# An encoder layer's merge: the sample's output product from the unsplit weight, row by row, and one turn of two tiles later

## The chip, the cores and the metric

The kernel runs on one core of a Trainium2 chip. The metric is the device time of one execution in microseconds (us), lower is better. Five engines work from queues of their own: TensorE (PE) multiplies into PSUM banks, VectorE (DVE), ScalarE (ACT) and GpSimd (POOL) do the elementwise work, and SyncE (SP) issues most of the transfers. Each engine takes its queue in order; semaphores hold an instruction back until its operands are there.

## The reference

One layer of an encoder for two groups: a prompt of 1024 tokens and a sample of 32 tokens with a cache of 512. What matters here is the end of the mixer and the beginning of the feed-forward part:

```python
merged = (g_a * (o_a.reshape(B, T, H_A * DV) @ w_proj_a)
          + g_b * (o_b.reshape(B, T, H_B * D_HB) @ w_proj_b))
x = x + gt1 * rms_norm(merged @ w_out, g_post_mix)
h2 = rms_norm(x, g_pre_ffn) * (1 + sc2) + sh2
f, new_conv = conv_ffn(h2, conv_state, w_up, conv_w, conv_b, w_down)
x = x + gt2 * rms_norm(f, g_post_ffn)
```

All data are float32 and the width is 1024. The change touches `merged @ w_out` for the 32 sample tokens, and the place of one transposition of normalised prompt rows for `h2 @ w_up`.

## The kernel before

The stages run in the order of `run` (L2188): `stage_merge` (L1509) follows the attention and precedes `stage_up` and `stage_down`.

**Precision.** A prompt product is made of three passes: each operand is split into a high and a low half (`hi` on ACT at L65, `lo` on DVE at L68), and `mm3` (L70) adds high x high, high x low and low x high. A sample product instead takes the operands as plain float32.

**The merge, row by row.** The merged activations are kept transposed, as eight rows `m` of 128 channels by 1056 tokens (1024 of the prompt, 32 of the sample at the end). The loop at L1532 makes for each `m`:

- the gates, loaded into tiles `t` and passed through a sigmoid (L1538, L1539), the branch B product loaded and multiplied in (L1544, L1545);
- the branch A product on PE, three blocks of 352 columns with twelve products each (`mtile`, L1550), multiplied by its gate and added (L1552, L1553);
- the split of the row into `mh` and `ml` (L1554, L1555), and a copy of its 32 sample columns into a tile `gs` (L1556, L1557), of which there are two buffers;
- the load of 128 rows of `w_out` into a tile `wr` (L1561) and its split into `dh`/`dl` (or `dr`) by `dsplit` (L1562). `wr` has two buffers for all weights of this stage: the branch A projections (L1367), `w_out` and the first up-projection weights (L1690).

**The output product of the prompt.** `natural` (L1434) makes, for token tile `t` and column half `h`, one bank `s` (three buffers) over a group of rows. Rows 0 and 1 come behind m=2 (their results are copied into the accumulators `facc`), rows 2 and 3 half behind m=4 and half behind m=6 (added to `facc` by DVE at L1460), rows 4 to 7 at the end (L1642). The last call begins the first three (t, h) with rows 4, 5 and 6, and adds row 7 to each of them afterwards.

**The output product of the sample.** `natural_s` (L1466) takes the copies `gs` as the small operand (128x32) and both halves of the split weight, read as float32, as the wide one. Its 1024 result columns are laid out as four blocks of 256 on partitions 0, 32, 64 and 96 of one bank, `pv` (one buffer). It is called three times: rows 0 and 1 (copied to `facc[8]`), rows 2 and 3 (added), rows 4 to 7 (added; called from `natural` after (t, h) = (1, 0)). Then `done(8)` (L1604) normalises the sample: ACT squares, PE sums over partitions (L321), POOL takes the root, DVE scales and adds the residual, and the same again for the next norm, up to the transposition at L1674.

**The turns.** `done(t)` (L1597) sums the squares of a finished prompt tile on ACT, `resid` (L1629) scales it and adds the residual, and leaves the normalised tile in `xn`. `turned(t0)` (L1586) is a generator: each of its two steps transposes half of the channels of two tiles on PE (`norm_2`, L1660) into two banks `tr` (two buffers), which ACT empties (L1666). A step is taken where `next` is called. After the last tile, `up_half` (L1711) begins the up-projection: four groups `(b, i)` of twelve products, in the order (0,0), (0,1), (1,0), (1,1), and after each it calls its function `then` (L1718). The step's PE instructions are bound to stand behind the product that was issued last (L1593).

**The order of the queues.** The kernel is written in a framework that traces the operations and then orders each engine's queue at compile time, by the order of the program and by estimates of when operands are ready; a later operation that is ready may be put ahead of an earlier one that isn't. `issue_after` binds an order by hand. So the position of an instruction in its queue follows from the program, buffers and estimates, and is fixed when the kernel runs.

Of the kernel before, what the change touches and what calls it, by code (L numbers as in the profile page):

```python
# [8 lines left out]
F32 = mybir.dt.float32  # L9
# [3 lines left out]
ALU = mybir.AluOpType  # L13
# [6 lines left out]
KT = 8  # L20
# [24 lines left out]
class K:  # L45
# [1417 lines left out]
                if (t, h) == (1, 0) and done:  # L1463
                    sample()

    def natural_s(self, facc, lhs, ws, first, done=None):  # L1466

        nc = self.nc
        ps = self.bank("pv")
        mm = [(x, w) for x, wl in zip(lhs, ws) for w in wl]  # L1470
        for i, (x, w) in enumerate(mm):
            for j in range(4):
                nc.tensor.matmul(ps[32 * j : 32 * j + 32, :256], x, w[:, j * 256 : j * 256 + 256],
                                 start=i == 0, stop=i == len(mm) - 1)
        if first:
            nc.scalar.copy(facc[8], ps[:, :256])
        else:
            nc.vector.tensor_tensor(facc[8], facc[8], ps[:, :256], ALU.add)
        if done:
            done(8)  # L1480

    def new_facc(self, pool):
        return [pool.tile([P, D] if t < 8 else [P, 256], F32, name=self.nm("facc")) for t in range(9)]
# [25 lines left out]
    def stage_merge(self):  # L1509
        nc, a = self.nc, self.a  # L1510
        E = self.E = self.tc.alloc_tile_pool(name="acc", bufs=1, reuse_waits="tile")
        facc = self.facc = self.new_facc(E)
        E3 = self.E3 = self.tc.alloc_tile_pool(name="work", bufs=2, reuse_waits="tile")
        m0 = [self.tl(E3, [P, T], F32R, g) for g in ("mh", "ml")]
        X = self.tc.alloc_tile_pool(name="m3", bufs=1, side="right", reuse_waits="tile")
        xh, xl = self.xh, self.xl
        lhs, lhs_s, ws = [], [], []

        def drop(n):
            del lhs[:n], lhs_s[:n], ws[:n]  # L1520

        def nat_s(n, first=False, done=None):
            b = lambda x: x.bitcast(F32)
            self.natural_s(facc, lhs_s[:n], [(b(h), b(l)) for h, l in ws[:n]], first, done)

        def nat(n, first=False, done=None):
            if not done:
                nat_s(n, first)
            self.natural(facc, lhs[:n], ws[:n], first, done, lambda: nat_s(n, first, done))
            drop(n)  # L1530

        for m in range(KT):  # L1532
            mc = slice(m * P, (m + 1) * P)
            h, l, banks = self.pa.pop(0) if self.pa else (*self.split_proj(self.w_proj_a(m) if m > 2 else self.w2), [])
            gs = []
            for s in (0, 1):
# [12 lines left out]
            banks = [(*b, ps) for b, ps in zip(blks, banks)]  # L1549
            for c0, n, ps in chain(banks, self.mtile(h, l, xh, xl, blks[len(banks) :], 4, {1: "tr", 2: "tr mm mm"}.get(m, "mm tr"))):  # L1550
                c = slice(c0, c0 + n)
                nc.vector.tensor_tensor(ga[:, c], ps[:, :n], ga[:, c], ALU.mult)  # L1552
            nc.vector.tensor_tensor(ga, ga, gb, ALU.add)  # L1553
            self.hi(mh, ga)  # L1554
            self.ml = self.lo(ml, ga, mh).ins  # L1555
            ms = self.tl(E3, [P, TS], F32, "gs")  # L1556
            nc.vector.tensor_copy(ms, ga[:, TP:T])  # L1557
            lhs.append((mh, ml))
            lhs_s.append(ms)
            raw = self.tl(self.W, [P, D], F32, "wr")  # L1560
            nc.sync.dma_start(raw, a["w_out"][0, mc])  # L1561
            ws.append(self.dsplit(E3, raw, "dh dl" if m % 4 < 3 else "dr dr"))  # L1562
            if m == 2:
                with self.tc.issue_after(self.pe):
                    nat(2, True)
            elif m in (4, 6):
                self.natural(facc, lhs[:2], ws[:2], False, tiles=range(2 * m - 8, 2 * m - 4))
                if m == 6:
                    nat_s(2, False)
                    drop(2)  # L1570
        X.release()
        self.Op.release()

        H = self.Hp = self.tc.alloc_tile_pool(name="h2", bufs=1, side="right", reuse_waits="tile")
        self.B1h, self.B1l, self.B2h, self.B2l = (H.tile([P, 4, HC], F32R, name=self.nm("B")) for _ in range(4))
        Fp = self.Fp = self.tc.alloc_tile_pool(name="h2f", bufs=1, side="right", reuse_waits="tile")
        self.f2 = Fp.tile([P, KT, HC], F32, name="f2")
        G = self.tl(E3, [P, UW], F32, "t")[:, :D]
        tmp = self.tl(E3, [P, UW], F32, "t")[:, :D]
        Gs = self.tl(E3, [P, 256], F32, "Gs")  # L1580
        xs, tmps = self.tl(E3, [P, 256], F32, "Gx", 1), self.tl(E3, [P, 512], F32, "hf")[:, :256]
        self.quarters(xs, a["x_sample"][0])
        self.gate_rows(0, "g_post_mix", G, Gs, tmp, tmps)
# [12 lines left out]

        def done(t, h=1):  # L1597
            f = facc[t]
            if self.turn2:
                if next(self.turn2, self) is self:  # L1600
                    self.turn2 = None
            if h == 0:
                return
            if t == 8:  # L1604
                self.post(f, self.rstd_s(f, E3), Gs, xs)
                nc.gpsimd.dma_start(self.x1s, f)
                nc.vector.tensor_scalar(xs, f, self.rstd_s(f, E3), None, ALU.mult)
                self.norm_2(8, [xs], E3)
                return
            rs.append(self.rstd(self.sumsq(f, P, E3, "jk", 512), D, P))  # L1610
            if t == 1:
                raw = [self.w_up(0), self.w_up(NCH)]
                with self.tc.issue_after(self.ml):
                    self.up_set = [self.wsplit(x) for x in raw]
            if t:
                with self.tc.issue_after(self.added[1]):
                    resid(t - 1)
                if t > 2 and t % 2:
                    self.turn2 = turned(t - 3)
            if t == 7:  # L1620

                first = ((self.B1h, self.B1l), (self.B2h, self.B2l))
                turn = self.turn2
                self.first = [self.up_half(self.up_set[0], first, ("mm", "mm"), lambda b, i: i and next(turn, None))]
                resid(7)
                turn = turned(6)
                self.first.append(self.up_half(self.up_set[1], first, ("s", "s"), lambda b, i: b + i == 1 and next(turn)))

        def resid(t):  # L1629
            f = facc[t]  # L1630
            x = self.tl(E3, [P, UW], F32, "t")[:, :D]
            nc.sync.dma_start(x, a["x_prompt"][0, t * P : (t + 1) * P])
            self.post(f, rs[t], G, x, None)
            nc.sync.dma_start(self.x1d[t], f)
            r = self.rstd(self.sumsq(f, P, E3, "jk", 512), D, P)
            if t < 6:
                self.hi(x, f, r)
            else:
                nc.vector.tensor_scalar(x, f, r, None, ALU.mult)
            xn.append(x)  # L1640

        nat(4, False, done)  # L1642
        E3.release()
        E.release()
# [608 lines left out]
```

## Time and profile before

| | |
|---|---|
| time, median of 3 runs (lowest to highest) | 1718.38 us (1718.2 to 1720.1) |
| the profiled execution's own time | 1721.95 us |
| its span | 1720.2 us |
| mean granted TensorE clock | 0.996 |

The span is the time from the first to the last instruction of the profiled execution; a chain or a timeline is read in times from its start. How busy PE, its weight loads (PEld), DVE, ACT and POOL are in three stretches of the stage, by the view of windows (us of busy time):

| stretch | length | PE | PEld | DVE | ACT | POOL | granted clock |
|---|---|---|---|---|---|---|---|
| 881 to 977: rows 1 to 7 and the output product's early parts | 96.0 | 94.92 | 79.30 | 65.99 | 43.83 | 0.75 | 1.00 |
| 977 to 1018.5: the last output products and the turns | 41.5 | 40.67 | 32.96 | 30.25 | 28.10 | 13.70 | 1.00 |
| 1018.5 to 1036: the first up products and the last turns | 17.5 | 16.21 | 15.62 | 12.60 | 13.51 | 6.52 | 1.00 |

In the rows of a timeline the columns are start, duration, engine, line, operation, result and operands, shape and count; a bracket gives the idle time of the engine before the instruction and what ended it. A matmul's duration there is its whole passage through the array; the next one may start before it has ended, so the distance from start to start is what a stream of them costs.

### The profile page before, as it was taken

What the parts mean: (1) busy time and instruction counts of PE and PEld (TensorE: products, weight loads), DVE (VectorE), ACT (ScalarE), POOL (GpSimd) and SP (SyncE); (2) the same over time, 40 slices, a digit from 0 to 9 for tenths busy, and PEclk for the clock granted to TensorE, in tenths of its full rate; (3) what the DMA queues carried; (4) which work ended last, traced back from release to release, by engine and by line L of the source; (5) the groups of instructions that cost most, each with busy time, mean ns of one, the idle gap of its engine ahead of it and who ended that gap; (6) DMA issues with size and microseconds to landing.
All of it is one profiled execution on the core that took longest, in us unless ns stands there. A gap on an engine that the chain in (4) does not pass through costs nothing. (4 is left out here: it accounts for less than half of the span.)

```text
span 1720.2 us, 29533 instructions
## 1 busy us (share of the span) xinstructions
PE 1681.7 (98%) x11444; PEld 1535.0 (89%) x11444; DVE 1201.8 (70%) x1960; ACT 904.3 (53%) x1730; POOL 276.0 (16%) x586
## 2 busy tenths in 40 slices
PE   6999999999999999999999999999999999999998
PEld 3899999999999989989789789999999999977886
DVE  4576475574663587878586679887787787788456
ACT  5455454454544677776683376444444444544442
POOL 2211111211110011111100131211121111110013
PEclk8999999999999999999999999999999999999999
DMA  8243333342431222222165530524323323697753
GB/s 324 81 132 108 106 110 87 97 127 74 135 117 56 80 80 74 65 61 73 63 255 157 176 135 26 178 93 129 129 93 130 129 93 129 228 338 243 233 150 120
DMA packets 169309, 224.15 MB, mean 130 GB/s; under 512 B 12901, under 2 KB 115504, under 8 KB 169168
## 3 DMA queue, kind: packets, MB, share of 16 engines
q1 hardware_dynamic: 153552, 178.43, 32.8%
q0 software_dynamic: 15392, 43.74, 7.2%
q8 instruction: 90, 1.47, 0.4%
q14 instruction: 51, 0.42, 0.1%
q10 hardware_dynamic: 224, 0.09, 0.0%
HBM read 169.92 MB, written 51.77 MB: 129 GB/s over the span
## 5 line engine op out<-in xcount | busy, mean ns | idle before, releaser
L65 ACT ACTIVATE wh<-wr 128x1024 fp32r<-128x1024 f32 (+6 forms) x156 | 131.6, 854 | 250.8 <-PE s L1707 78.0
L68 DVE TENSOR_TENSOR wl<-wr,wh 128x1024 fp32r<-128x1024 f32 (+5 forms) x153 | 149.1, 981 | 129.1 <-ACT wh L65 129.0
L72 PE MATMUL mm<-hh,wh 128*128 128x352 f32 x688 | 232.0, 337 | 0.0
L73 PE MATMUL mm<-hl,wh 128*128 128x352 f32 x688 | 224.4, 326 | 0.4 <-DVE hl L291 0.4
L74 PE MATMUL mm<-hh,wl 128*128 128x352 f32 x688 | 224.4, 326 | 0.0
L72 PEld LDWEIGHTS mm<-hh,wh 128*128 128x128 f32 x688 | 130.3, 189 | 8.9 <-issue 4.9
L73 PEld LDWEIGHTS mm<-hl,wh 128*128 128x128 f32 x688 | 130.2, 189 | 3.8 <-DVE hl L291 1.7
L74 PEld LDWEIGHTS mm<-hh,wl 128*128 128x128 f32 x688 | 129.9, 189 | 0.8 <-issue 0.8
L68 DVE TENSOR_TENSOR PTl<-tr,PTh 128x512 fp32r<-128x512 f32 x96 | 65.6, 687 | 46.4 <-ACT PTh L65 45.7
L1706 PE MATMUL s<-T,wh 128*128 128x256 f32 (+1 forms) x328 | 93.5, 285 | 0.4 <-DVE u L1783 0.3
L1708 PE MATMUL s<-T,wl 128*128 128x256 f32 (+1 forms) x328 | 93.6, 285 | 0.0
L1707 PE MATMUL s<-T,wh 128*128 128x256 f32 (+1 forms) x328 | 93.2, 284 | 0.0
L1847 DVE SCALAR_TENSOR_TENSOR u<-u,c,u 128x1058 f32<-128x1058 f32 x68 | 87.1, 1318 | 2.0 <-ACT u L1844 0.7
L591 PE MATMUL tr<-c,A 128*128 128x128 f32 x576 | 83.8, 273 | 1.0 <-DVE os L1357 0.3
L65 ACT ACTIVATE PTh<-tr 128x512 fp32r<-128x512 f32 x96 | 57.0, 598 | 49.0 <-PE tr L591 48.9
L1708 PE MATMUL tr<-T,wl 128*128 128x272 f32 (+1 forms) x272 | 77.7, 285 | 0.4 <-DVE wl L68 0.4
L1706 PE MATMUL tr<-T,wh 128*128 128x272 f32 (+1 forms) x272 | 77.8, 286 | 0.0
L1707 PE MATMUL tr<-T,wh 128*128 128x272 f32 (+1 forms) x272 | 77.4, 285 | 0.0
L591 PEld LDWEIGHTS tr<-c,A 128*128 128x128 f32 x576 | 68.1, 140 | 6.4 <-issue 1.8
L68 DVE TENSOR_TENSOR wl<-S,wh 128x1024 fp32r<-128x1024 f32 x40 | 49.0, 1224 | 35.1 <-ACT wh L65 35.1
L1708 PE MATMUL mm<-T,wl 128*128 128x256 f32 (+1 forms) x256 | 73.0, 286 | 0.3 <-DVE wl L68 0.2
L1706 PE MATMUL mm<-T,wh 128*128 128x256 f32 (+1 forms) x256 | 73.1, 286 | 0.0
(688 smaller groups left out, 5341.7 us busy)
## 6 DMA issues: line engine op xcount, KB each, us to landing
wr<-in_w_ada_dram SPq DMA_DIRECT2D x48, 512.0 KB, 4.7
wr<-in_w_up_dram SPq DMA_DIRECT2D x44, 512.0 KB, 4.2
dr<-in_w_down_dram SPq DMA_DIRECT2D x43, 512.0 KB, 5.7
wr<-in_w_in_dram SPq DMA_DIRECT2D x33, 512.0 KB, 4.5
wr<-gdn SPq DMA_DIRECT2D x30, 512.0 KB, 4.2
gdn<-u POOLq DMA_DIRECT2D x23, 512.0 KB, 5.4
gd<-nat POOLq DMA_DIRECT2D x48, 176.0 KB, 2.3
t<-gd SPq DMA_DIRECT2D x16, 528.0 KB, 5.2
```

The costliest lines, as they stand in the source:

```text
L65: self.nc.scalar.activation(out, in_, AF.Identity, scale=scale)
L68: return self.nc.vector.tensor_tensor(out, full, hi.bitcast(F32), ALU.subtract)
L72: m(ps, lh, rh, start=start, stop=False)
L73: m(ps, lh, rl, start=False, stop=False)
L74: self.pe = m(ps, ll, rh, start=False, stop=stop).ins
L591: self.nc.tensor.transpose(tr[:, (2 * s + q) * P : (2 * s + q + 1) * P], at[q][:, b * P : b * P + P], self.idt)
L1706: m(ps[:, :n], w[0][:, k], x[0][:, k, c], start=first and k == 0, stop=False, skip_group_check=True)
L1707: m(ps[:, :n], w[0][:, k], x[1][:, k, c], start=False, stop=False, skip_group_check=True)
L1708: i = m(ps[:, :n], w[1][:, k], x[0][:, k, c], start=False, stop=k == 3, skip_group_check=True)
L1847: nc.vector.scalar_tensor_tensor(y, u[:, w : w + YW], self.cvT[:, w, cc : cc + 1], y, ALU.mult, ALU.add)
```

## The change

1. The sample's output product uses the loaded float32 tile `wr` itself instead of its two halves. It is made in eight parts, one for each row `m` directly behind the load of its weight, all into one bank `pv` that stays open from m=0 to m=7. The calls for groups of rows, the two additions to `facc[8]` and the early copy go; one copy of the finished bank to `facc[8]` on ACT comes, at the place where the last group was called.
2. In the first `up_half`, the two steps of the turn of tiles 4 and 5 are taken after groups (1,0) and (1,1) instead of (0,1) and (1,1): the first of them twelve products later.

```diff
-    def natural_s(self, facc, lhs, ws, first, done=None):
-
-        nc = self.nc
-        ps = self.bank("pv")
-        mm = [(x, w) for x, wl in zip(lhs, ws) for w in wl]
-        for i, (x, w) in enumerate(mm):
-            for j in range(4):
-                nc.tensor.matmul(ps[32 * j : 32 * j + 32, :256], x, w[:, j * 256 : j * 256 + 256],
-                                 start=i == 0, stop=i == len(mm) - 1)
-        if first:
-            nc.scalar.copy(facc[8], ps[:, :256])
-        else:
-            nc.vector.tensor_tensor(facc[8], facc[8], ps[:, :256], ALU.add)
-        if done:
-            done(8)
+    def natural_s(self, m, x, w):
+
+        if m == 0:
+            self.ns = self.bank("pv")
+        for j in range(4):
+            self.nc.tensor.matmul(self.ns[32 * j : 32 * j + 32, :256], x, w[:, j * 256 : j * 256 + 256],
+                                  start=m == 0, stop=m == KT - 1)
...
+        def sample():
+            nc.scalar.copy(facc[8], self.ns[:, :256])
+            done(8)
 
         def nat(n, first=False, done=None):
-            if not done:
-                nat_s(n, first)
-            self.natural(facc, lhs[:n], ws[:n], first, done, lambda: nat_s(n, first, done))
-            drop(n)
+            self.natural(facc, lhs[:n], ws[:n], first, done, sample)
+            del lhs[:n], ws[:n]
...
             raw = self.tl(self.W, [P, D], F32, "wr")
             nc.sync.dma_start(raw, a["w_out"][0, mc])
+            self.natural_s(m, ms, raw)
             ws.append(self.dsplit(E3, raw, "dh dl" if m % 4 < 3 else "dr dr"))
...
                 if m == 6:
-                    nat_s(2, False)
-                    drop(2)
+                    del lhs[:2], ws[:2]
...
-                self.first = [self.up_half(self.up_set[0], first, ("mm", "mm"), lambda b, i: i and next(turn, None))]
+                self.first = [self.up_half(self.up_set[0], first, ("mm", "mm"), lambda b, i: b and next(turn, None))]
```

More of the change, by code (lines that the diff above doesn't have):

```diff
@@ L1516, in stage_merge @@
         xh, xl = self.xh, self.xl
[L1517 to L1524, printed above, removed]
+        lhs, ws = [], []
+        def sample():
+            nc.scalar.copy(facc[8], self.ns[:, :256])
+            done(8)
         def nat(n, first=False, done=None):
-            if not done:
-                nat_s(n, first)
-            self.natural(facc, lhs[:n], ws[:n], first, done, lambda: nat_s(n, first, done))
-            drop(n)
+            self.natural(facc, lhs[:n], ws[:n], first, done, sample)
+            del lhs[:n], ws[:n]
         for m in range(KT):
@@ L1558, in stage_merge @@
             lhs.append((mh, ml))
-            lhs_s.append(ms)
             raw = self.tl(self.W, [P, D], F32, "wr")
             nc.sync.dma_start(raw, a["w_out"][0, mc])
+            self.natural_s(m, ms, raw)
             ws.append(self.dsplit(E3, raw, "dh dl" if m % 4 < 3 else "dr dr"))
```

## The prediction

> **What bounds the kernel now.** I read the page's busy shares first, then the time order of TensorE (PE) through the merge stage, 881 to 1036 us, then its waits in that stretch.
>
> ```profile
> span 1720.2 us, 29533 instructions
> ```
>
> ```profile
> PE 1681.7 (98%) x11444; PEld 1535.0 (89%) x11444; DVE 1201.8 (70%) x1960; ACT 904.3 (53%) x1730; POOL 276.0 (16%) x586
> ```
>
> PE is busy for 98% of the span, so what counts is how long PE's queue is and where PE stands in it. Work taken off the vector engine (DVE) or ScalarE (ACT) is worth something only where PE waits for it.
>
> ```profile
> PE tr L1660 <- ACT t L65: 0.9, 1, 0.9
> PE s L74 <- DVE ml L68: 0.7, 1, 0.7
> PE tr L321 <- ACT hf L319: 0.5, 1, 0.5
> ```
>
> These are the three longest entries of PE's waits between 866 and 1045 us. The first is the transposition that the last hunk of the change moves. The second is the first product of row m=7, waiting for its low half. The third belongs to the sample's normalisation. Three small waits in 180 us: the stage is a nearly unbroken stream of products, and the sum has to come from the stream.
>
> **The change part by part.**
>
> *The sample's product.* Its instructions now, grouped by operand:
>
> ```profile
> L1473 PE MATMUL pv<-dh,gs x48: 379/379/404, 885.3 to 975.3; 128*32 128x256 f32 x48
> L1473 PE MATMUL pv<-dl,gs x48: 379/379/379, 885.7 to 975.7; 128*32 128x256 f32 x48
> L1473 PE MATMUL pv<-dr,gs x32: 379/379/379, 956.4 to 976.6; 128*32 128x256 f32 x32
> ```
>
> 48 + 48 + 32 = 128 instructions. The code has 8 rows m, two weight halves (high and low) and four column blocks, 64 calls, so each float32 call is two instructions. After the change each row multiplies the loaded weight once: 32 calls, 64 instructions. The 379 ns are not the price, since four blocks run in the array side by side; the price is the distance from one eight to the next:
>
> ```profile
> 973.13 0.61 PE L1473 MATMUL pv<-dl,gs 128*32 128x256 f32 x8
> 973.56 0.61 PE L1473 MATMUL pv<-dh,gs 128*32 128x256 f32 x8
> 974.00 0.61 PE L1473 MATMUL pv<-dl,gs 128*32 128x256 f32 x8
> 975.01 0.42 PE L1473 MATMUL pv<-dh,gs 128*32 128x256 f32 x4 [0.40 <-DVE gs L1557]
> ```
>
> Two eights lie between 973.13 and 974.00, so 0.87 / 16 = 0.054 us for one instruction. The 64 that go are worth 64 x 0.054 = 3.5 us.
>
> But entering and leaving the 32-column form costs something each time. A block of sixteen:
>
> ```profile
> 884.84 0.32 PE L73 MATMUL mm<-V,wh 128*128 128x352 f32 x1
> 885.00 0.32 PE L74 MATMUL mm<-V,wl 128*128 128x352 f32 x1
> 885.25 0.64 PE L1473 MATMUL pv<-dh,gs 128*32 128x256 f32 x8
> 885.71 0.61 PE L1473 MATMUL pv<-dl,gs 128*32 128x256 f32 x8
> 886.25 0.50 PE L72 MATMUL s<-dh,mh 128*128 128x512 f32 x1
> 886.59 0.39 PE L73 MATMUL s<-dl,mh 128*128 128x512 f32 x1
> 886.82 0.39 PE L74 MATMUL s<-dh,ml 128*128 128x512 f32 x1
> ```
>
> A product of 352 columns takes 0.16 us to the next start (884.84 to 885.00), one of 512 columns 0.23 (886.59 to 886.82). Without the block, the second product after it would have started at 885.00 + 0.16 + 0.23 = 885.39; it started at 886.59. The block cost 1.20 us, of which 16 x 0.054 = 0.86 is work and 0.34 is the two changes. The new blocks have eight instructions of the very form that the conditioning product already runs alone:
>
> ```profile
> 343.42 0.64 PE L203 MATMUL mm<-wr,cT 128*32 128x256 f32 x8
> 343.99 0.43 PE L72 MATMUL mm<-hh,wh 128*128 128x352 f32 x1
> 344.26 0.32 PE L73 MATMUL mm<-hl,wh 128*128 128x352 f32 x1
> ```
>
> 0.57 to the next start, 0.27 - 0.16 = 0.11 more to the one behind, and the 0.09 of entering seen above (885.25 against 885.16): 0.77 us, that is 0.43 of work and again 0.34. Now the stage has four blocks: two of sixteen (m = 0 and 1), one of 32 (m = 2, 3) and one of 64 (m = 4 to 7) with a wait in its middle. Afterwards each row is ready at another time, so I count eight. Four more blocks cost 4 x 0.34 = 1.4 us. Net: -3.5 + 1.4 = **-2.1**.
>
> That each change of form costs 0.34 us is measured above. The Trainium skill has a rule that speaks against this change here: changing the tiling mode, and not just the tile, drains TensorE (TensorEngine Tiling (Array Packing), Key Properties). It gives no price; by it every one of the eight blocks pays on both sides, however short, as the rows show for eight and for sixteen. Had the finer cut cost nothing, the net of this part would be -3.5.
>
> *The wait in the middle.* In the rows above, the eight at 975.01 should have started at 974.43: 0.58 us late, waiting for the copy of a sample row (gs). That tile has two buffers, both held by rows 4 and 5 until the products at 972 to 974. In the new form a row's product runs right behind its copy and the buffers come free early. **-0.6.**
>
> *The wait for m=7.* PE stood 0.7 us before that row's third product. Up to there it had done three sample blocks, 64 x 0.054 + 3 x 0.34 = 4.5 us; afterwards it will have done seven or eight, 5.4 or 6.2 us. PE comes 0.9 to 1.7 us later to a wait of 0.7. The low half itself gets no later:
>
> ```profile
> 967.18 1.06 ACT L65 ACTIVATE wh<-wr 128x1024 fp32r<-128x1024 f32 x1 [2.19 <-DMA wr<-in_w_up_dram]
> 968.15 1.07 ACT L65 ACTIVATE mh<-t 128x1056 fp32r<-128x1056 f32 x1
> ```
>
> The high half of row 7 (mh) stands in ACT's queue behind the split of the second up-projection weight, which waits 2.19 us for its load. That load will come later (below) and its split falls behind mh. **-0.7.**
>
> *New waits.* Each of the eight blocks now follows directly on a copy of DVE's, and PE is in order: where DVE is late, the projection and output products behind wait too. Below lies 0. Above, the largest wait of the stage, 0.9, eight times: 7.2. The nearest row is L1473 itself: five starts now, one of them 0.58 late. 8 / 5 x 0.58 = **+0.9** is the value I take.
>
> *The held weight buffer.* The loaded float32 tile (wr, two buffers, shared with the projection and up weights) is now read by PE, so it stays until the row's sample copy exists; so far it went free after the split.
>
> ```profile
> 903.81 0.38 SPq L1367 DMA_DIRECT2D wr<-in_w_proj_a_dram  x1
> ...
> 960.12 0.38 SPq L1690 DMA_DIRECT2D wr<-in_w_up_dram  x1
> ```
>
> ```profile
> 918.23 0.17 DVE L1557 COPY gs<-t 128x32 f32<-128x32 f32 x1
> ```
>
> ```profile
> DMA to landing us min/median/max: 3.4/3.9/6.0
> ```
>
> The projection weight of m=5 went out at 903.81. With both buffers held by w_out of rows 3 and 4 it goes out when row 3's sample copy (918.23) has been used, near 919; with at most 6.0 to land and some 1.4 to split it is there by 926.5, and PE's products of m=5 begin here:
>
> ```profile
> 932.65 0.32 PE L72 MATMUL mm<-QH,wh 128*128 128x352 f32 x1
> ```
>
> Rows 6 and 7 have room of the same kind. What is late is the second up weight: it needs the buffer of w_out 7, so it goes out near 969 in place of 960.12. Its products come in the second up half, just ahead of the turn at 1030.12 shown further below. I cost the hold at nothing, covered by these margins; the case without cover is a rival below. The loads queued behind it on SyncE (gain rows, residual rows) keep their own order of readiness and are no earlier than now.
>
> *The open bank.* The sum stays in bank pv from row 0 to the copy:
>
> ```profile
> L605 PE MATMUL pv<-ptd,V x256: 277/281/481, 96.2 to 872.9; 128*128 128x256 f32 x128
> ```
>
> The attention's last use of it starts at 872.9, before row 0's block, and the stage asks for it nowhere else: nothing. Two DVE adds and one early ACT copy go, one late ACT copy comes; neither engine bounds PE there.
>
> *The transposition twelve products later.*
>
> ```profile
> 1021.38 0.27 PE L1660 MATMUL tr<-c,t 128*128 128x128 f32 x1
> 1022.52 0.33 PE L1660 MATMUL tr<-c,t 128*128 128x128 f32 x1 [0.87 <-ACT t L65]
> ...
> 1024.81 1.91 ACT L1666 ACTIVATE f<-tr,c,c 128x256 f32<-128x256 f32 x4
> ...
> 1029.19 0.75 DVE L1639 TENSOR_SCALAR t<-facc,rs 128x1024 f32<-128x1024 f32 x1 [1.00 <-POOL rs L98]
> ...
> 1030.12 0.27 PE L1660 MATMUL tr<-c,t 128*128 128x128 f32 x1
> ```
>
> Twelve products of 0.12 us put these transpositions near 1022.9, and tile 5, ready at 1022.5, is no longer waited for. But PE then has only twelve products, not twenty-four, before the second half of the same turn, which needs the two tr banks that ACT empties from 1024.81 to 1026.7; and behind that, tile 7 is ready at 1029.94 for transpositions that now start at 1030.12. Both lie on ACT, DVE and GpSimd and don't move. The 0.9 becomes two smaller waits: I take **0**, with -0.9 and +0.5 as ends (another half microsecond if the banks are freed in a worse order).
>
> **The sum.** -2.1 - 0.6 - 0.7 + 0.9 + 0 = -2.5 us. The profiled execution took 1721.95 us, its span is 1720.2; it would become 1719.5. The median shown is 1718.38, 3.6 below the profiled one; the same 2.5 off gives **1715.9**. That is 0.15%; about 0.2%, or 3.4 us, is what a measurement of this kernel can tell from no change.
>
> **The rivals.**
>
> *All of it pays.* No block waits, and PE's earlier arrival at the turn is used. For it: few waits in this stage, seven of eight turns without one now. Against it: tile 7's chain. -2.1 - 0.6 - 0.7 - 0.9 = -4.3: 1714.1.
>
> *The wait takes the place of the work.* Every block finds its copy 0.58 late, as the one at 975.01: 8 x 0.58 = 4.6 in place of 0.9: +1.2, 1719.6. For it: the copies stand in DVE's queue among whole-row operations. Against it: four of five starts have no such wait.
>
> *The held buffer stops the tail: slower.* The second up weight goes out near 969. The load of 960.12 was used at 967.18, 7.0 us later; so ACT splits it from 976 and DVE ends the low half near 978.2. If that split keeps its place in DVE's queue, ahead of the output product's additions, the first of three s banks comes free at 978.9, while PE, past (0,0), (0,1) and (1,0), wants a fourth bank. Now it takes it here:
>
> ```profile
> 976.87 0.50 PE L72 MATMUL s<-dh,mh 128*128 128x512 f32 x1
> ```
>
> Without the block of 64 and its wait (64 x 0.054 + 0.34 + 0.58 = 4.4) that is 972.5, with up to 1.7 for the earlier blocks and without the 0.7 it is 973.5: 5.4 us of standing, and with ACT's squares behind the same load about a microsecond more. -2.5 + 6.5 = +4.0: 1722.4. It decides from about 6 us of standing. Against it: the order of a queue is set by estimated readiness, so the split should move behind the additions; only an estimate several microseconds short would leave it there.
>
> *It doesn't do what it says*: blocks could fall together again. Each pair saves 0.34, so even four pairs give -3.9, 1714.5, and this counts with the first rival.
>
> **How the numbers follow.** Forecast 0.47, all pays 0.25, wait in place of work 0.16, held buffer 0.12. Around the forecast the spread of the waits (0 to 2) goes from -3.4 to -1.4, and a sixth of it may pass -3.4: 0.08 goes to faster. Faster by over 0.2%: 0.25 + 0.08 = 0.33. Slower: 0.12. Within: 0.55. The range takes in the first rival with a little room (1713.3) and the second (1719.6), and leaves out the held buffer and the far edge of the first, together under 2 in 10.
>
> **What would show it.** Right: 64 instructions on the sample product in eight blocks near 0.77 us; no wait of PE for gs longer than 0.6; none for ml; the transposition near 24 + 12 products without its 0.87, and a new wait at the next turn or at tile 7. Wrong: blocks with waits of half a microsecond each; ACT or DVE standing for the up weight while PE waits for s banks; or later stages in another order than now, which this sum leaves out.

## The result, and the profile after

The changed kernel takes 1722.44 us (median of 22 executions), the kernel before 1719.88 us (median of 22, measured beside it). The ratio is 1.0016, with a 95% interval of 1.0009 to 1.0023. Three later measurements gave 1.0004 (0.9995 to 1.0013), 1.0010 (1.0001 to 1.0019) and 1.0013 (1.0004 to 1.0022); the mean of the four is 1.0011, or 1.9 us. So the change makes the kernel slower by about a tenth of a per cent. The forecast was 1715.9 us, faster by 2.5. Of the 6.5 us between forecast and result, 1.5 are the base (the three times shown gave 1718.38 for before, 22 give 1719.88), 2.5 are the gain that did not come, and the rest is a loss that was not foreseen.

The page of the profile after. Its execution took 1721.36 us, 1.1 below the median of its kernel; that of the profile before took 1721.95, 2.1 above. So these two traces alone do not show the loss:

```profile
span 1719.6 us, 29413 instructions
...
PE 1679.8 (98%) x11380; PEld 1532.2 (89%) x11380; DVE 1201.8 (70%) x1958; ACT 903.9 (53%) x1730; POOL 280.0 (16%) x586
```

11444 instructions of PE have become 11380: the 64 are gone. PE is busy 1.9 us less, and the span is 0.6 us shorter. GpSimd (POOL) does the same 586 instructions in 4.0 us more. That small number is where the trail below leads.

The four longest of PE's waits from 866 to 1045 us in the trace after (total, times, longest):

```profile
PE tr L1646 <- ACT f L1652: 1.1, 2, 0.8
PE tr L1646 <- ACT hf L1652: 1.1, 2, 0.8
PE tr L321 <- ACT hf L319: 0.6, 2, 0.4
PE tr L1660 <- DVE Gx L1593: 0.5, 1, 0.5
```

Lines behind the changed code stand 14 lower than before (L1646 is the transposition that was L1660). The waits for ml, for gs and for tile 5 are gone. In their place stand two waits of a new kind: PE has the tile, but the bank that the transposition needs has not been emptied by ACT. One of them is at the second step of the turn of tiles 4 and 5, at 1025 us, as the prediction had it; the other is in the first turn, at 1000 us, where before had none. A wait of 0.3 us for the high half of row 1 is new as well.

### The profile page after: what moved, and what is told of

Read it like the earlier page. It is cut to its first block, busy times and chain, and to the rows that moved or that the text cites. A ratio compares the mean times of both kernels' runs of the same rounds, so it can differ in the third digit from the quotient of the medians.

```text
span 1719.6 us, 29413 instructions
## 1 busy us (share of the span) xinstructions
PE 1679.8 (98%) x11380; PEld 1532.2 (89%) x11380; DVE 1201.8 (70%) x1958; ACT 903.9 (53%) x1730; POOL 280.0 (16%) x586
```

## Where the time went

*The blocks came out as forecast.* Row 0's block in PE's timeline after, and the group of all eight:

```profile
883.88 0.32 PE L72 MATMUL mm<-KH,wh 128*128 128x352 f32 x1
884.13 0.64 PE L1471 MATMUL pv<-wr,gs 128*32 128x256 f32 x8
884.70 0.43 PE L73 MATMUL mm<-KL,wh 128*128 128x352 f32 x1
884.97 0.32 PE L74 MATMUL mm<-KH,wl 128*128 128x352 f32 x1
```

```profile
L1471 PE MATMUL pv<-wr,gs x64: 379/391/403, 884.1 to 967.0; 128*32 128x256 f32 x64
```

From 883.88 to 884.97 are 1.09 us, where two plain products take 2 x 0.16: the block cost 0.77, the forecast figure, 0.43 of them work. 64 instructions in eight blocks, none waiting in this trace.

*PE did reach the turns 2.5 us earlier.* All traces start differently (the first 45 us, which wait for loads, differ by up to 3.6 us between executions of the kernels here), so I compare stretches, called the stage from here on: from the start of one of PE's last products of the attention, near 870 us, to the start of the sixteenth product behind the turn of tiles 4 and 5, near 1029 us. In a second trace of before these start at 869.98 and 1028.96: the stage is 158.98 us long. In its first trace it is 159.17. In three of four traces of the changed kernel it is 158.91, 158.89 and 158.86: no shorter. But up to the last product ahead of 1000 us the same three traces are ahead of that second trace of before by 2.5 to 2.6 us, as the sum said. The gain was there, and was lost between 1000 and 1029 us. The first place, in PE's timeline after and before:

```profile
998.80 0.40 PE L74 MATMUL s<-dr,ml 128*128 128x512 f32 x1
1000.01 0.66 PE L1646 MATMUL tr<-c,t 128*128 128x128 f32 x4 [0.82 <-ACT hf L1652]
1000.92 0.66 PE L1646 MATMUL tr<-c,t 128*128 128x128 f32 x4 [0.26 <-ACT hf L1652]
```

```profile
1002.05 1.04 PE L1660 MATMUL tr<-c,t 128*128 128x128 f32 x8
```

Before, the second step of this turn took its eight transpositions in one piece; now it stands twice. PE is 2.5 us ahead in front of this step and 1.0 behind it, and 0.8 behind the second turn. The second place is the turn of tiles 4 and 5: the wait for tile 5 is gone, which gives 0.8, but the turn's second step takes 1.5 more than before, and 0.1 is left:

```profile
1025.29 0.66 PE L1646 MATMUL tr<-c,t 128*128 128x128 f32 x4 [0.84 <-ACT f L1652]
1026.20 0.66 PE L1646 MATMUL tr<-c,t 128*128 128x128 f32 x4 [0.25 <-ACT f L1652]
```

*Why ACT was not earlier at the first turn.* ACT empties the banks (hf) in its own order, behind the scaling of tile 2 (t), which needs that tile's rs from GpSimd. ACT's timeline after:

```profile
990.84 0.19 ACT L105 ACTIVATION_READ_ACCUMULATOR jk<-facc 128x1 f32 x1
...
993.77 1.15 ACT L65 ACTIVATE t<-facc,rs 128x1024 f32<-128x1024 f32 x1 [1.56 <-POOL rs L98]
...
995.77 0.19 ACT L105 ACTIVATION_READ_ACCUMULATOR jk<-facc 128x1 f32 x1
...
997.90 1.15 ACT L65 ACTIVATE t<-facc,rs 128x1024 f32<-128x1024 f32 x1 [1.94 <-POOL rs L98]
998.96 1.91 ACT L1652 ACTIVATE hf<-tr,c,c 128x256 f32<-128x256 f32 x4
```

and before:

```profile
993.01 0.19 ACT L105 ACTIVATION_READ_ACCUMULATOR jk<-facc 128x1 f32 x1
994.14 1.15 ACT L65 ACTIVATE t<-facc,rs 128x1024 f32<-128x1024 f32 x1 [0.94 <-POOL rs L98]
...
997.33 0.19 ACT L105 ACTIVATION_READ_ACCUMULATOR jk<-facc 128x1 f32 x1
998.46 1.15 ACT L65 ACTIVATE t<-facc,rs 128x1024 f32<-128x1024 f32 x1 [0.94 <-POOL rs L98]
999.52 1.92 ACT L1666 ACTIVATE hf<-tr,c,c 128x256 f32<-128x256 f32 x4
```

From the end of a row's sum of squares to its scaling: before 994.14 - 993.20 = 0.94 and 998.46 - 997.52 = 0.94; after 993.77 - 991.03 = 2.74 and 997.90 - 995.96 = 1.94. The two gaps are 1.8 and 1.0 us longer. So the chain was 2.2 us ahead of before at the first sum (990.84 against 993.01) and only 0.6 at hf; 0.3 of either is this stage's earlier start, and ACT has one sum less to do between the two steps, or nothing would be left. GpSimd's two small operations lie in those gaps. GpSimd's timeline after, and DVE's beside it:

```profile
984.09 0.55 POOL L98 TENSOR_TENSOR rs<-rv,c 128x1 f32<-128x1 f32 x1
...
991.11 1.01 POOL L97 TENSOR_SCALAR rv<-ss 128x1 f32<-128x1 f32 x1 [0.36 <-ACT jk L105]
992.20 1.53 POOL L98 TENSOR_TENSOR rs<-rv,c 128x1 f32<-128x1 f32 x1
...
996.32 1.55 POOL L98 TENSOR_TENSOR rs<-rv,c 128x1 f32<-128x1 f32 x1
```

```profile
983.87 0.68 DVE L1460 TENSOR_TENSOR facc<-facc,s 128x512 f32<-128x512 f32 x1
...
990.79 1.28 DVE L1498 SCALAR_TENSOR_TENSOR facc<-facc,rs,t 128x1024 f32<-128x1024 f32 x1
992.11 1.23 DVE L1499 TENSOR_TENSOR facc<-facc,t 128x1024 f32<-128x1024 f32 x1
...
996.18 1.28 DVE L1498 SCALAR_TENSOR_TENSOR facc<-facc,rs,t 128x1024 f32<-128x1024 f32 x1
```

Both operations work on one column. The second (L98) takes 0.55 us when it runs alone and 1.53 when DVE has just begun one of its residual operations, which read two tiles of SBUF: it ends 0.4 us after DVE's (993.73 against 993.34, 997.87 against 997.46). The first (L97) takes 0.19 alone, and here 1.01: it ends 0.05 us after DVE's (992.12 against 992.07). Beside DVE's addition from a bank (983.87) the second takes 0.55. Before, the same two steps begin ahead of DVE's operation and take 0.19 and 0.55:

```profile
993.28 0.19 POOL L97 TENSOR_SCALAR rv<-ss 128x1 f32<-128x1 f32 x1 [0.36 <-ACT jk L105]
993.56 0.55 POOL L98 TENSOR_TENSOR rs<-rv,c 128x1 f32<-128x1 f32 x1
```

```profile
993.65 1.28 DVE L1506 SCALAR_TENSOR_TENSOR facc<-facc,rs,t 128x1024 f32<-128x1024 f32 x1
```

The Trainium skill names the rule (SBUF — State Buffer, SBUF: two separate sides): DVE's second pair of ports is shared with GpSimd, as an exclusive lock for a whole instruction, and an operation of DVE with two SBUF inputs takes it. The trace agrees as to GpSimd's waiting, the case with a bank among the inputs too. That DVE would in its turn wait for GpSimd these rows do not show: DVE's operation at 993.65 begins while GpSimd's of 993.56 runs, and takes the 1.28 us of the others. Between 974 and 1031 us, 4 of GpSimd's small operations take over 1.0 us in both traces of before, 7 in all four of the changed kernel. Three of the seven are those above, and they cost 0.8 + 1.0 + 1.0 = 2.8 us in the chain of the first turn.

*What stands ahead of it.* The second up weight, in the buffer that the sample's product now holds. Its load goes out at 967.48 in place of 960.12. In SyncE's, ACT's and DVE's timelines after:

```profile
967.48 0.38 SPq L1676 DMA_DIRECT2D wr<-in_w_up_dram  x1
```

```profile
972.45 1.06 ACT L65 ACTIVATE wh<-wr 128x1024 fp32r<-128x1024 f32 x1 [4.63 <-DMA wr<-in_w_up_dram]
...
975.40 1.06 ACT L105 ACTIVATE jk<-facc 128x1024 bf16<-128x1024 f32 x1 [1.89 <-DVE facc L1460]
```

```profile
972.26 0.69 DVE L1460 TENSOR_TENSOR facc<-facc,s 128x512 f32<-128x512 f32 x1 [2.36 <-PE s L74]
973.54 1.23 DVE L68 TENSOR_TENSOR wl<-wr,wh 128x1024 fp32r<-128x1024 f32 x1 [0.60 <-ACT wh L65]
974.68 1.28 DVE L1460 TENSOR_TENSOR facc<-facc,s 128x512 f32<-128x512 f32 x2
```

DVE does one addition, waits for the split of that weight, and only then the second: tile 0's squares start at 975.40, though PE was ahead. Before, they start here:

```profile
974.30 1.06 ACT L105 ACTIVATE jk<-facc 128x1024 bf16<-128x1024 f32 x1 [5.08 <-DVE facc L1460]
```

Counted from the start of the stage (869.56 after, 869.88 before) they are 1.4 us later than before. From there DVE, GpSimd and ACT meet in another phase. That this late start is what brings GpSimd's steps behind DVE's is read from the order of the rows; it is argued, not shown.

## Experiments

Two theories stood against each other at first: H, the held buffer makes the tail's chain late; T, that chain is full and gives PE's gain back whatever the loads do. A third, P (the collisions of GpSimd with DVE give PE's gain back), came later, from the first eight traces.

| kernel | ratio to before (95%) | stage, us | GpSimd over 1 us |
|---|---|---|---|
| before, two traces | 1 | 159.17, 158.98 | 4, 4 |
| changed, four traces | 1.0016, 1.0004, 1.0010, 1.0013 | 158.91, 158.89, 158.86, 159.86 | 7, 7, 7, 7 |
| sample's product alone | 1.0014 (1.0005–1.0023) | 160.13 | 7 |
| transposition alone | 1.0003 (0.9994–1.0012) | 159.84 | 4 |
| before, buffer held | 1.0023 (1.0013–1.0032) | 161.85 | 3 |
| before, four gs buffers | 1.0001 (0.9992–1.0010) | 160.29 | 4 |
| changed, from the high half | 0.9992 (0.9983–1.0001), 0.9998 (0.9989–1.0007) | 158.29, 157.68 | 2, 2 |
| changed, up split later | 1.0007 (0.9997–1.0017), 0.9999 (0.9989–1.0008) | 157.74, 160.26 | 3, 3 |
| changed, residual in halves | 0.9989 (0.9980–0.9998), 0.9997 (0.9988–1.0006) | 157.56, 160.97 | 0, 0 |
| changed, both | 0.9990 (0.9979–1.0001), 0.9990 (0.9981–0.9999) | 155.85, 154.83 | 2, 2 |
| before, residual in halves | 0.9998 (0.9989–1.0007) | 159.07 | 0 |

A stage is that of one execution, a ratio that of 9 to 22; they need not agree. Differences of 0.1% are near what these runs can tell apart, so I lean on those that came twice.

**Both kernels again**, unchanged.

> The changed kernel once more, for a second trace and more times. Its median stood 2.6 us above the one of before, but its one trace is 0.6 us shorter, so something differs between executions. Theory A (the gain is given back at the turns, nothing else): the second trace again shows PE 3 us earlier at the end of the merge products, 2.4 us of it lost at the turns by 1027 us, and the time within 1 us of before. Theory B (the weight buffer held by the sample's product makes loads go out late, so that in some executions a landing is waited for): this trace or its times spread upward, with ACT or PE waiting 1 to 4 us longer for a weight load between 920 and 975 us. Theory C (the place is elsewhere, the granted clock or the start): the offset to before appears before 880 us or after 1100 us.

> The kernel before once more, for a second trace. Its first trace was 1721.95 us against a median of 1719.9. All theories: near 1720, and the stretch in which it is 2 us shorter than the first trace shows where executions of the same kernel differ. Theory A and B expect the merge stage (880 to 1036 us) to be of equal length within 0.5 us in both traces; Theory C expects the difference in the start or in the granted clock.

The stage has the same length in both kernels, and the loss sits at the turns in each trace of the changed one: A of the expectation holds for the traces. The trace of before that was to be 2 us shorter was not; most of the difference between executions lies in the first 45 us.

**The two parts alone.** The changed kernel with `lambda b, i: i and next(turn, None)`, and the kernel before with `lambda b, i: b and next(turn, None)`.

> The sample's product row by row from the loaded weights, the transposition left in its old place after 24 products. Theory A: the three us gained reach the turns and are given back there as well (the old place has the 0.9 us wait for tile 5, now longer since PE comes earlier), so within 1 us of the changed kernel. Theory B: the same 2.6 us slower than before as the whole change. If the moved transposition were what costs, this kernel is faster than before by 1 to 3 us.

> The kernel before with only the transposition twelve products later. Theory A: the 0.9 us wait before it goes and about as much comes at the next step of the same turn: within 0.5 us of before. Theory B: the same, since no buffer is touched. If the moved transposition were what costs, this one is slower than before by 2 us or more.

The sample's product alone is as slow as the whole change (1.0014); the transposition alone (1.0003) cannot be told from before. PE's timeline of the latter:

```profile
1024.26 0.66 PE L1660 MATMUL tr<-c,t 128*128 128x128 f32 x4 [0.43 <-ACT f L1666]
1025.17 0.66 PE L1660 MATMUL tr<-c,t 128*128 128x128 f32 x4 [0.26 <-ACT f L1666]
```

The wait for tile 5 is gone and the banks are waited for instead; the turn as a whole costs PE what it costs in before, to within 0.1 us. In the kernel with the sample's product alone, tile 5 is waited for 1.6 us, and this turn takes 0.7 more than in before, as it does in the changed kernel: in either place the transposition ends up waiting for the same engines. The stage of the transposition alone is 0.9 longer by a wait of 0.5 for ACT near 905 us and small ones, far from the turn.

**The held buffer, taken away and put in.** High half only:

```diff
-            self.natural_s(m, ms, raw)
             ws.append(self.dsplit(E3, raw, "dh dl" if m % 4 < 3 else "dr dr"))
+            self.natural_s(m, ms, ws[-1][0].bitcast(F32))
```

Held, in the kernel before:

```diff
             ws.append(self.dsplit(E3, raw, "dh dl" if m % 4 < 3 else "dr dr"))
+            nc.gpsimd.tensor_tensor(self.tl(E3, [P, 1], F32, "hold", 1), raw[:, :1], ms[:, :1], ALU.add)
```

> The changed kernel, but the sample's product reads the high half of the split weight (it leaves out the low half) in place of the loaded weight: the same 64 instructions in eight blocks, and the loaded weight is no longer held. Two traces of the changed kernel show PE 2.5 us ahead after the products' first tiles and none of it left at 1029 us: the squares of the first tile start at 974.4 us, no earlier than before, since DVE's split of the second up weight (loaded from 966.5 in place of 960) stands ahead of the additions. Theory H (held buffer): here that load goes out near 958 to 960 again, the additions run from 971 without it, the squares of tile 0 start 1.5 us earlier or more, and the merge stage (offset between 870 and 1029 us) is 1.5 us shorter or more. Theory T (the turns' chain over DVE, GpSimd and ACT is full whatever the loads do): the load goes out early and the stage is still within 0.4 us of before.

> The kernel before, with one added GpSimd operation of one column per row that reads the loaded output weight and the row's sample copy, so that the buffer is held until that copy exists, as in the change, while TensorE's work stays. Theory H: the second up weight's load goes out after 965 us, the additions are late and the merge stage is 1 to 3 us longer than before. Theory T: within 0.5 us of before, the turns having the room.

> The sample's product from the high halves (the low half left out), a second time: same work of TensorE as the change, buffer not held. Its trace had two long GpSimd operations in place of seven. Held buffer and collisions as the cause: again 0.999 of before, some 0.2% below the changed kernel. If the first figure (0.9992) was a draw, 1.000 or more.

With the hold, the kernel before is 0.23% slower; its up weights go out at 972.63, and tile 5 is waited for 1.6 us in place of 0.9. Without the hold, the changed kernel is at 0.9992 and 0.9998 in place of 1.0011.

But the first of these edits did more than hold a buffer. PE's queue came out in another order: 36 products of a branch A projection stand some 18 us later, behind output products, and the sample's product is cut into six blocks instead of four. 1.6 us of the 2.9 by which its stage is longer lie ahead of the first turn, where PE waits no longer than in before; and the long GpSimd operations are 3. So this run does not show what the hold alone costs, and a held buffer by itself does not bring the seven long operations.

Without the hold, neither theory's figure came: the stages are 0.7 and 1.3 us shorter than before's (H: 1.5 or more; T: within 0.4). H is wrong in the detail: with the load out at 959.61, DVE splits both up weights ahead of all additions, as it does in before, and tile 0's squares start no earlier; PE stands 1.5 us for a bank in that trace instead. What came with the hold's end was the number of long GpSimd operations, 2 in place of 7.

**The sample copies' buffers**, in the kernel before: `"gs": 4`.

> The kernel before with four buffers for the sample copies in place of two and nothing else, which takes away the 0.4 to 0.6 us wait of the sample's product near 975 us. Theory H: the 0.6 us is kept, since nothing in the loads gets later: stage 0.4 to 0.6 us shorter. Theory T: PE gets to the turns 0.6 us earlier and waits 0.6 us longer there: stage within 0.2 us.

The wait of the sample's product is gone and this came in its place, in PE's waits:

```profile
PE s L72 <- DVE facc L1460: 1.6, 1, 1.6
```

PE came early to banks that DVE, at its splits, had not emptied. The stage is 1.3 us longer than in before, which neither theory said, and the time is the same (1.0001). It is the lesson of the whole change in small.

**The second up weight's split later**, in the changed kernel:

```diff
                 with self.tc.issue_after(self.ml):
-                    self.up_set = [self.wsplit(x) for x in raw]
+                    self.up_set = [self.wsplit(raw[0])]
+            if t == 2:
+                with self.tc.issue_after(self.added[1]):
+                    self.up_set.append(self.wsplit(raw[1]))
```

> The changed kernel with the split of the second up weight put behind the third tile's additions in the code, so that DVE does the first tiles' additions without waiting for it; the buffer stays held and the load stays late. Theory H: the additions run when PE is done with them, the squares of tile 0 start at 972.5 or before in place of 974.4, the stage is 1 to 2 us shorter than that of the changed kernel, and the time 1 to 2 us below it. Theory T: the stage's length is unchanged within 0.4 us.

> The changed kernel with the second up weight's split behind the third tile's additions, a second time: its trace was 1.2 us shorter in the merge stage than the changed kernel's, its median (over 11 scattered times) was not. Held buffer as the cause: stage again 1.0 to 1.3 us shorter than that of the changed kernel, and the median 0.5 to 2 us below it on the same chip.

In the first trace the first turn waits 0.2 in place of 1.1 and the stage is 1.2 shorter, though tile 0's squares start at 974.0 and not at 972.5: ACT's split of that weight still stands ahead of them. The buffer is still held in this kernel, and the long GpSimd operations are 3. In the second trace the stage is 2.5 us longer than in the first, by a wait of 1.3 us of one of the sample's blocks for its copy and one of 1.1 us in the sample's normalisation (L321). The ratios, 1.0007 and 0.9999, do not tell it from the changed kernel with certainty.

**The residual in halves**, in the changed kernel and with the edit above:

```diff
-            self.post(f, rs[t], G, x, None)
+            for h in (0, 512):
+                self.post(f[:, h : h + 512], rs[t], G[:, h : h + 512], x[:, h : h + 512], None)
```

> The changed kernel with the two DVE operations of the residual done in halves of 512 columns. In the traces a GpSimd operation of 0.55 us takes 1.53 when a DVE operation with two inputs of 1024 columns starts just before it; in the changed kernel's tail seven operations of 42 are such, in before four, and the three more stand in the chain of the turns. Theory P (these collisions give the gain back): none of GpSimd's small operations in the tail takes over 1.0 us, the turn waits at 1000 us (0.82 and 0.26) are smaller by half a microsecond or more, and the stage is 0.5 to 1.5 us shorter than that of the changed kernel. Against it: DVE's order of work changes as well and each half costs some 0.05 us more, so the stage stays within 0.4 us or gets longer.

> Both edits: the second up weight's split later, and the residual's operations in halves. If the late split and the collisions are two separate losses, the stage is 1.5 to 2.5 us shorter than that of the changed kernel and 1.3 to 2.3 shorter than before's, the time 1 to 2 us below before. If they are one (the late additions cause the collisions), it is as the later split alone, 1.2 us.

> The changed kernel with the residual in halves, a second time, beside the next and the one above on one chip. Theory P: again about 0.999 of before.

> Both repairs, a second time. If they take away what the change lost: ratio to before 0.999 or so again, some 0.2% below the changed kernel on the same chip. If the first was a draw: 1.000.

With halves alone no operation of GpSimd takes over 1.0 us and no turn waits for ACT, but PE is also later at the first turn, by waits of 1.1 us (L321) and 0.5 (a bank): that trace is no clean proof of P. In the second trace, loads that came late cost 2.3 and 1.0 us around 906 and 953, and the time, 0.9997, is not the 0.999 that P expected. With both edits the gain stays. PE's waits in the second trace of that kernel, the longest three:

```profile
PE tr L321 <- ACT hf L319: 0.5, 1, 0.5
PE tr L1650 <- DVE t L1629: 0.5, 1, 0.5
PE s L1698 <- DVE wl L68: 0.4, 1, 0.4
```

and the two steps of GpSimd in the first turn, then that turn on PE:

```profile
992.10 0.19 POOL L97 TENSOR_SCALAR rv<-ss 128x1 f32<-128x1 f32 x1 [2.31 <-ACT jk L105]
992.38 0.55 POOL L98 TENSOR_TENSOR rs<-rv,c 128x1 f32<-128x1 f32 x1
```

```profile
993.99 1.04 PE L1650 MATMUL tr<-c,t 128*128 128x128 f32 x8
997.65 1.04 PE L1650 MATMUL tr<-c,t 128*128 128x128 f32 x8
```

PE comes 3.1 us earlier than in the second trace of before (to 997.65 from the stage's start, 128.91 against 132.00), the turn takes it without a wait, and the stage ends 4.2 us earlier. It was 0.9990 of before twice: 1718.10 and 1717.88 us against 1720.37 and 1720.19. This version is below both kernels on both occasions (the changed kernel took 1721.87 and 1722.48 us beside it), though against before by no more than 0.1%, with intervals that end at 1.0001 and 0.9999. Of the 3.1 and 4.2 us that its two traces gain, 2.8 and 2.0 are lost again by 1100 us: 0.8 in each at tile 7, which is now the late one, and most of the rest to a wait for the low half of an up weight (1.8 and 1.0).

**Is halving worth the same without the change?**

> The kernel before with DVE's residual operations in halves and nothing of the change. In its trace the turns have one wait of 0.9 us, and the long GpSimd operations (four) do not stand in the chain of a turn that waits. Theory P (the change moved the small operations into collisions, and these gave its gain back): nothing to win here, ratio to before 0.9995 to 1.0005, stage within 0.5 us. Rival (halving is worth the same in any version): ratio 0.998 to 0.999, stage 1 us shorter or more.

The time says no: 0.9998. The trace says less. Its stage is as long as before's, but not because nothing happened: the wait of 0.9 us for tile 5, the one turn of before that waits, is gone; PE is 1.1 us later ahead of the first turn, and behind the stage, at tile 7, another 0.6 goes. So halving is worth something at the turns of before too, and costs it elsewhere; that it repairs only what the change broke is not shown.

**The changed kernel twice more.**

> The changed kernel a third time, on the same chip as the next three, since two measurements of it gave +0.16% and +0.04% against before. If the ratio is 1.0010 or so again, both are draws of one small loss; its trace should have, as the two earlier ones, seven GpSimd operations over 0.9 us in the tail and the merge stage within 0.4 us of before.

> The changed kernel a fourth time. If the waits of the sample's blocks for their row's copy come only in some executions, its trace has none (as three before it) or one of 1 us or more, and the ratio is again 1.0005 to 1.0016. A fourth trace without any leaves them unshown for this kernel.

The third has the seven long operations and a stage of 158.86 us, as expected. The fourth trace has the wait that the other three lack:

```profile
951.06 0.64 PE L1471 MATMUL pv<-wr,gs 128*32 128x256 f32 x8 [1.08 <-DVE gs L1544]
```

Its cause, in ACT's and DVE's timelines of that trace:

```profile
947.79 0.63 ACT L65 ACTIVATE wh<-wr 128x512 fp32r<-128x512 f32 x1 [1.22 <-DMA wr<-in_w_proj_a_dram]
```

```profile
948.45 0.69 DVE L68 TENSOR_TENSOR wl<-wr,wh 128x512 fp32r<-128x512 f32 x1 [1.41 <-ACT wh L65]
949.06 1.25 DVE L1540 TENSOR_TENSOR t<-t,t 128x1056 f32<-128x1056 f32 x1
...
950.83 0.17 DVE L1544 COPY gs<-t 128x32 f32<-128x32 f32 x1
```

The projection weight of row 7, issued at 942.8 into a buffer that had been held (in before at 930.3), landed 1.2 us after ACT wanted it; DVE's split stood ahead of row 6's sum, and the block behind that sum waited. The stage of this trace is 1.0 us longer than those of the other three.

## Why the prediction was wrong, step by step

- **64 instructions less, four more blocks: -2.1.** Right: 64 instructions, eight blocks, none merged with another, and 0.77 us for the one shown. (The 0.34 in it is for going into the 32-column form and out again together.)
- **The wait of the sample's product: -0.6; the wait for m=7: -0.7.** Both are gone, the first but for the new kind of wait in the next point. But the second was read off one execution: it is 0.7 us in the first trace of before and 0.3 in its second.
- **New waits of the blocks for their copies: +0.9.** Too high, and not a steady price: 0 in three traces, 1.1 in the fourth, 0.3 in the mean.
- **The sum up to the first turn: -2.5.** Right in size, 2.5 to 2.6 in the three traces without that wait and 1.6 in the fourth, but in part by luck: in those three the 0.9 was not paid, the wait for m=7 gave 0.3 in place of 0.7 against the second trace of before, and 0.3 for row 1's high half and 0.3 more in the sample's normalisation were not in the sum.
- **The transposition: 0.** Right: one wait of 0.9 for two of 0.4 to 0.8 and 0.3. What this turn loses in the changed kernel, 0.7, it loses in either place.
- **The held buffer, costed at nothing.** Wrong. Its three margins were counted for landings in one execution, and for PE alone. They held in three traces, and in the fourth that of row 7 did not; the second up weight stood, as the third rival said, among DVE's additions. The rival's price (PE standing for banks) was not paid, in any trace of the changed kernel. What was paid is that the additions and all behind them came no earlier.
- **The step that failed** is the one that carries -2.1 - 0.6 - 0.7 to the end of the stage without asking who else has to be early. I gave a price only to the turn of tiles 4 and 5 and to tile 7 behind it, since seven of eight steps had no wait. The runs show the gain of 2.5 us in front of the first turn's second step, and of it 1.5 lost in that step, 0.2 at the second turn and 0.7 at the turn of tiles 4 and 5. A turn without a wait does not say how much room it has. Each tile reaches its turn over DVE, ACT, GpSimd, DVE, ACT, GpSimd and ACT, and that chain starts with DVE's additions. At the first turn it had 1.9 us of PE's 2.5 (2.2 less the earlier start), and GpSimd's operations, running into DVE's, took 2.8.

Shown: that the gain exists in front of the first turn and is gone at 1029 us, and where it goes; that GpSimd's operations take 2.8 us longer in the chain of the first turn; that the gain stays, and more, when the late split and the long DVE operations are taken away together; that the sample's product alone is as slow as the whole change, in one measurement. Only argued: that the late second up weight is what shifted the chain into the collisions. Taking the hold away removed most of them, but changed the order of DVE's work too; and with the buffer held, the kernel before has 3 of them and the changed kernel with the later split 3. Open: how much of the 2.5 us the collisions alone cost, since halving alone moved other waits too. Open as well: the traces explain why nothing was won, and one wait in one trace of four explains a fraction of a microsecond; of the 1.9 us by which the times lie above before's, the larger part is not pinned to a place. It is not the granted clock, which is 0.9963 in the mean of the executions of the changed kernel that the three later ratios rest on and 0.9964 in that of the executions of before beside them.

## What to carry to other kernels

Work taken off the busiest engine ends where the next transfer of tiles between engines is no earlier than before; so before counting the gain, follow one tile through all its engines up to the point where the busiest engine needs it, and read the slack there, not the absence of a wait. Small operations of GpSimd in such a chain are cheap only as long as DVE isn't working on two SBUF tiles at that moment; shorter operations of DVE shorten that wait, though halving them cost time in other places here. And a buffer that is held longer moves the loads of everything that shares it: ask of each load what stands behind it in the order of the engine that first touches it.

## What the runs showed of the hardware

- GpSimd's operation L98, on one column, ends 0.4 us after a DVE operation of two SBUF inputs within which it begins: 0.55 us become 1.53 to 1.55 in the rows after. Within an operation of 512 columns in place of 1024 it takes 0.88 to 0.94 (the kernel with both edits). L97 ends 0.05 us after DVE's: 0.19 become 1.01. The other way round nothing shows: in the 19 traces here 60 of DVE's residual operations of 1024 columns begin, by the profile's spans, while one of these GpSimd operations runs, and they take 1.21 to 1.28 us like the others.
- The first 45 us of the program, which wait for the first loads, differ by up to 3.6 us between single executions (0 to -3.55 against the second trace of before). Two traces of this kernel are not to be compared by their spans.
